# A diffusion layer on one core: the FFN's sums of weights move from VectorE to adding transfers

## The chip, the cores and the metric

The program runs on one core of a Trainium2 chip. A core has a matrix engine (PE, TensorE), a vector engine (DVE, VectorE), a scalar engine (ACT, ScalarE), a general engine (POOL, GpSimd) and a queue engine (SP, SyncE) that here only starts transfers. Sixteen DMA engines carry all transfers of the core. Weights lie in DRAM, tiles in SBUF (128 partitions), products in PSUM. The metric is the device time of one execution in microseconds, as the median of several runs.

## The reference, cut to what matters

One layer is computed for 384 tokens (128 context tokens, 256 latent tokens) of width 2048, all in float32. After a mixing half, which the change doesn't touch, comes a dense SwiGLU feed-forward part (FFN) with 5632 hidden columns:

```python
h = rmsnorm(x, lw['norm_pre_ffn']) * (1.0 + sc2) + sh2
ff = (jax.nn.silu(h @ lw['w_ffn_gate']) * (h @ lw['w_ffn_up'])) @ lw['w_ffn_down']
x = x + ga2 * rmsnorm(ff, lw['norm_post_ffn'])
```

## The kernel before, in words

**Precision.** A float32 product is made of three products of a shorter format (float32r): every operand is split in a high part `hi`, a rounded copy, and a low part `lo = x - hi`, and the kernel forms hi·hi + hi·lo + lo·hi. For weights, ACT makes `whi` (a cast, line 1385) and DVE makes `wlo` (a subtraction, line 1396). Each such weight piece is 128 partitions x 1024 floats, 512 KB.

**The FFN.** The hidden columns are taken in 11 chunks (`NFC`) of 512 columns. The first chunk is made plainly. For chunks 1 to 10 the tokens form three blocks of 128, and the gate and up products of blocks 1 and 2 are made by a scheme of Strassen's kind: seven products of sums of weights with sums of activations instead of eight products. Block 0 is made plainly. The activation sums (`S1` to `S4`) are made once; the weight sums are made for every chunk. A chunk consists of *kinds* of steps, each of four steps i = 0..3 (one quarter of the half of the inner length that the kind works on):

| kind | weights that it multiplies | products of 512 columns in a step |
|---|---|---|
| A | up weights, first half of the inner length | 12 |
| B | gate weights, first half | 12 |
| C | gate weights, second half | 12 |
| E | C - (B - A) | 6 |
| F | C - B | 6 |
| G | up weights, second half | 12 |
| H | G - (C - (B - A)) | 6 |
| D | down weights of the chunk before (eight steps) | 18 |

The list `steps` (line 1308) writes out their order by hand. Before, it is A0..A3, B0..B3, then four times C, E, D, then four times F, G, H, D.

**Where the weights lie.** The pieces of C, G and D are loaded into `raw`, which has two buffers. Those of A and B are loaded into eight places `slots`, tiles named `u...` (shown as `u` in the profile): `x`, the place of A(i), and `y`, the place of B(i). Sums are made in place: x becomes B - A (`sum1`, line 1369), then C - x (line 1392), then G - x (line 1395); y becomes C - y (line 1393). E and H multiply what stands in x, F what stands in y. When F and H have been split, their places are free for the next chunk's loads.

**Order of the work.** For every step, `grab2` takes the split weights of the step from the list `ready`, starts loads (`load_more`: SP, lines 1355 and 1363), and splits the weights of a later entry (`split_next`: the ACT cast, then up to three pending evictions, then the sums, then the DVE subtraction). `whi` and `wlo` have four buffers each, one in use and three ahead: a step's cast can begin when the product step four places ahead of it in the list has ended. All engines execute their instructions strictly in the program's order. SP, too, waits in order: a load into `raw` or into a place waits until DVE has made the `wlo` that read the old contents. A further generator, `ada_last`, loads 64 pieces of 256 KB in the same stage (line 1422) and multiplies them on DVE (line 1427).

Of the kernel before, what the change touches and what calls it, by code (L numbers as in the profile page):

```python
# [15 lines left out]
ALU = mybir.AluOpType  # L16
# [5 lines left out]
D = 2048  # L22
# [12 lines left out]
FC = 4  # L35
NFC = FT // FC
G = 1024
# [59 lines left out]
def tile_step(ctx: ExitStack, tc: tile.TileContext, a, o):  # L97
    nc = tc.nc
    PE, ACT, DVE, POOL, SP = nc.tensor, nc.scalar, nc.vector, nc.gpsimd, nc.sync
# [74 lines left out]
    def down_src(c, n, kh):  # L174

        return a["w_d"][c, 2 * n : 2 * n + 2, :, 512 * kh : 512 * kh + 512].rearrange("i p x -> p i x")
# [429 lines left out]
    with ExitStack() as s:  # L606
# [203 lines left out]
        for c in range(2):  # L810

            dst = a2.rearrange("p (h d j) -> p d h j", d=2, j=P)[:, c]
            raw, up = (x.rearrange("p (h j) -> p h j", j=P) for x in (raw3[1 + c][0:98, 0:512], part[0:98]))
# [28 lines left out]
    with ExitStack() as s:  # L842
# [158 lines left out]
        for b, i in mix_order:  # L1001
# [9 lines left out]
            else:  # L1011
# [3 lines left out]
                p = psm.tile([P, T], F32, tag="mm", name="pmm")  # L1015
                gemm(p, grab(hold=True), oT, 8)
                g, y = gates.pop((b, i))
# [14 lines left out]
    with ExitStack() as s:  # L1032
# [49 lines left out]
        for i in range(KT):  # L1082
            p = psm.tile([P, T], F32, tag="mm", name="pmm")
            for g in range(2):
                n = 2 * i + g - 2 * KT
# [164 lines left out]
        for q in range(2):  # L1250
# [12 lines left out]
        slots = [t[:, n, :] for t, k in (  # L1263
            (actp.tile([P, 3, G], F32, tag="C_hi", name="u012"), 3), (actp.tile([P, 3, G], F32, tag="C_lo", name="u345"), 3),
            (adap.tile([P, 2, G], F32, tag="adacc", name="u67"), 2),
        ) for n in range(k)]
# [41 lines left out]
        steps = []  # L1308
        for c in range(1, NFC):
            steps += [("A", c, i) for i in range(4)] + [("B", c, i) for i in range(4)]  # L1310
            for i in range(4):
                steps += [("C", c, i), ("E", c, i), ("D", c - 1, i)]
            for i in range(4):
                steps += [("F", c, i), ("G", c, i), ("H", c, i)] + ([("D", c - 1, 4 + i)] if c < NFC - 1 or i < 2 else [])
        steps += [("D", NFC - 2, 6 + i) for i in range(2)]
        d_order = (0, 2, 1, 3)
        steps += [("D", NFC - 1, 2 * n + k) for n in d_order for k in range(2)]
# [1 line left out]
        def gu_src(kind, c, half, i):  # L1319
            return a["w_" + kind][FC * c : FC * c + FC, half, :, 256 * i : 256 * i + 256].rearrange("n p x -> p n x")  # L1320

        def src_of(kind, c, i):
            if kind == "D":
                return down_src(c, i // 2, i % 2)
            return gu_src(*{"A": ("u", c, 0), "B": ("g", c, 0), "C": ("g", c, 1), "G": ("u", c, 1)}[kind], i)
# [16 lines left out]
        def slot(x, c, i):  # L1342

            return 4 * ((c + x) % 2) + i
# [19 lines left out]
                resident.pop(0)  # L1364
                kept -= 1

        def sum1(c, i):
            x, y = (slots[slot(n, c, i)] for n in range(2))
            DVE.tensor_sub(x, y, x)  # L1369

        def settle_pend():
            for _ in range(3):
                if pend:
                    pend.pop(0)()

        def split_next():

            if not entries:
                settle_pend()
                return  # L1380
            kind, c, i, raw = entries.pop(0)
            x, y = (slots[slot(n, c, i)] if kind not in "RD" else None for n in range(2))
            src = raw if kind in "RCGD" else y if kind == "F" else x
            hi, lo = (wp.tile([P, G], F32R, tag=t, name=t, bufs=4) for t in ("whi", "wlo"))
            ACT.copy(hi, src)  # L1385
            settle_pend()
            if (kind, i) == ("A", 3):
                sum1(c, 0)
            elif kind == "B" and i < 3:
                sum1(c, i + 1)  # L1390
            elif kind == "C":
                DVE.tensor_sub(x, raw, x)
                DVE.tensor_sub(y, raw, y)
            elif kind == "G":
                DVE.tensor_sub(x, raw, x)
            DVE.tensor_sub(lo, src, hi.bitcast(F32))  # L1396
            if kind in "RCGD":
                out_now[0] -= 1
            elif kind == "F":
                free.add(slot(1, c, i))  # L1400
            elif kind == "H":
                free.add(slot(0, c, i))
            ready.append((hi, lo))

        def grab2(kept=2):
            w = take()
            while now:
                now.pop(0)()
            load_more(kept)
            split_next()  # L1410
            return w
# [52 lines left out]
        for u in range(HEAD):  # L1464
            kind, c, j = ffn_order[u]
            dst_of[kind](hp[u], c, j)
        n = 0
        for kind, c, j in ffn_order[HEAD:]:
            p = psm.tile([P, T], F32, tag="mm", name="pmm")
# [98 lines left out]
        for kind, c, i in steps:  # L1568
# [8 lines left out]
            if kind == "D":  # L1577
                w = grab2()
                n, kh = i // 2, i % 2
# [57 lines left out]
        n = d_order[-1]  # L1637
# [144 lines left out]
```

## Time and profile before

| what | before |
|---|---|
| median of 3 runs | 1968.85 us (1968.83 to 1969.1) |
| the profiled execution | 1969.33 us |
| its span, first to last instruction | 1967.6 us |
| first to last step of chunks 1 to 10 | 973.7 to some 1913 us of the span, 94 us per chunk |
| PE busy, whole span | 1951.9 us (99%) |
| DVE busy | 1620.2 us (82%) |
| ACT busy | 905.7 us (46%) |
| POOL busy | 32.2 us (2%) |
| moved by DMA | 380.08 MB, 193 GB/s on the mean |

The span is the profiled execution between its first and last instruction; the rest, 1.7 us, lies around it. "Busy" counts the time in which an engine executes something; a wait line "A <- B" says that A's engine stood idle until B released it. In a table of windows, the columns after the window are its length, then for each engine the busy time and the number of instructions, then the granted clock of PE (1.00 is full), the mean busy share of the 16 DMA engines and what they moved.

### The profile page before, as it was taken

To read this page: it belongs to the slowest core of one execution; us is meant where nothing else is said; L and a number is where in the kernel's file an instruction comes from. 1 tells how busy PE (TensorE), PEld (TensorE's weight loads), DVE (VectorE), ACT (ScalarE), POOL (GpSimd) and SP (SyncE) were. 2 spreads that over 40 slices of the span, in tenths; PEclk is the share of its full clock that TensorE was granted. 3 is DMA by queue.
4 is the path that set the end of the run, shared out by engine and by line. 5 is a ranking of instruction groups with operands and counts; after the bars stand their busy time and mean duration, and the time that the engine had idled before them with its cause. 6 is when DMAs were issued, how large, how long until landed. Compare 5 with 4: busy or idle time off the path is not lost.

```text
span 1967.6 us, 27720 instructions
## 1 busy us (share of the span) xinstructions
PE 1951.9 (99%) x10704; PEld 1731.7 (88%) x10704; DVE 1620.2 (82%) x2043; ACT 905.7 (46%) x1265; POOL 32.2 (2%) x44
## 2 busy tenths in 40 slices
PE   8999999999999999999999999999999999999998
PEld 6779999999999999999988888888888888888886
DVE  5569788878767778877789998999898999887875
ACT  4233454544345645446454444444444444444444
POOL 0000000000000000004000000000000000000001
PEclk9999999999999999999999999999999999999999
DMA  9978677767755697655345445463636363626243
GB/s 388 372 257 275 211 255 238 234 218 246 238 183 182 197 312 222 196 171 203 119 136 186 149 140 162 154 188 118 193 127 205 100 209 103 208 75 193 75 161 128
DMA packets 189412, 380.08 MB, mean 193 GB/s; under 512 B 14172, under 2 KB 112668, under 8 KB 184928
## 3 DMA queue, kind: packets, MB, share of 16 engines
q1 hardware_dynamic: 189136, 377.92, 59.0%
q8 instruction: 84, 1.38, 0.3%
q14 instruction: 48, 0.39, 0.1%
q10 hardware_dynamic: 144, 0.39, 0.1%
HBM read 361.48 MB, written 16.78 MB: 192 GB/s over the span
## 4 chain that ended last, share of the span: by engine, by line
PE 96%; DMA 1%; DVE 1%; ACT 1%; issue 0%; SPq 0%; POOL 0%; DVEq 0%; ACTq 0%; POOLq 0%
PE pmm L252 35%; PE pgu L1484 30%; PE pdn L1484 18%; PE pv L392 3%; PE pf L252 2%; PE pgm L375 1%; DMA slab<-in_w_ada 1%; PE px L410 1%; PE pmm L1238 1%; PE ptr L1545 1%; PE po L639 1%; DMA raw<-in_w_d 0%; PE pr L574 0%; PE dl L639 0%; PE pp L869 0%; PE px L883 0%
## 5 line engine op out<-in xcount | busy, mean ns | idle before, releaser
L252 PE MATMUL pmm<-A_hi,whi 128*128 128x384 f32 x1200 | 404.2, 337 | 0.0
L252 PE MATMUL pmm<-A_hi,wlo 128*128 128x384 f32 x1200 | 401.3, 334 | 0.0
L252 PE MATMUL pmm<-A_lo,whi 128*128 128x384 f32 x1200 | 401.2, 334 | 0.0
L1385 ACT CAST whi<-u 128x1024 fp32r<-128x1024 f32 x200 | 210.6, 1053 | 275.7 <-DVE u L1369 86.2
L1385 ACT CAST whi<-raw 128x1024 fp32r<-128x1024 f32 x175 | 184.2, 1053 | 209.7 <-DMA raw<-in_w_g 69.8
L218 ACT CAST whi<-raw 128x1024 fp32r<-128x1024 f32 x181 | 189.9, 1052 | 182.4 <-DMA raw<-in_w_gate 59.6
L219 DVE TENSOR_TENSOR wlo<-raw,whi 128x1024 fp32r<-128x1024 f32 x179 | 218.0, 1222 | 66.9 <-ACT whi L218 66.5
L1396 DVE TENSOR_TENSOR wlo<-u,whi 128x1024 fp32r<-128x1024 f32 x200 | 244.2, 1221 | 29.3 <-ACT whi L1385 16.7
L1484 PE MATMUL pgu<-whi,A_hi 128*128 128x512 f32 x640 | 250.0, 391 | 0.0
L1484 PE MATMUL pgu<-whi,A_lo 128*128 128x512 f32 x640 | 249.3, 389 | 0.0
L1396 DVE TENSOR_TENSOR wlo<-raw,whi 128x1024 fp32r<-128x1024 f32 x175 | 213.5, 1220 | 32.3 <-ACT whi L1385 22.7
L252 PEld LDWEIGHTS pmm<-A_hi,whi 128*128 128x128 f32 x1200 | 225.3, 188 | 2.5 <-issue 1.4
L252 PEld LDWEIGHTS pmm<-A_lo,whi 128*128 128x128 f32 x1200 | 225.4, 188 | 0.2
L252 PEld LDWEIGHTS pmm<-A_hi,wlo 128*128 128x128 f32 x1200 | 225.3, 188 | 0.0
L566 DVE SCALAR_TENSOR_TENSOR adacc<-adaw,spad,adacc 128x1024 f32<-128x1024 f32 x180 | 222.8, 1279 | 1.0 <-DMA adaw<-in_w_ada 0.7
L1484 PE MATMUL pdn<-whi,hid_hi 128*128 128x512 f32 x480 | 186.9, 389 | 0.0
L1484 PE MATMUL pdn<-whi,hid_lo 128*128 128x512 f32 x480 | 186.8, 389 | 0.0
L1484 PE MATMUL pgu<-wlo,A_hi 128*128 128x512 f32 x640 | 184.2, 389 | 0.0
L1484 PEld LDWEIGHTS pgu<-whi,A_hi 128*128 128x128 f32 x640 | 120.1, 188 | 26.1 <-issue 0.8
L1484 PEld LDWEIGHTS pgu<-wlo,A_hi 128*128 128x128 f32 x640 | 120.1, 188 | 25.4
L1484 PEld LDWEIGHTS pgu<-whi,A_lo 128*128 128x128 f32 x640 | 120.2, 188 | 25.0
L1484 PE MATMUL pgu<-whi,S 128*128 128x512 f32 x480 | 131.1, 395 | 0.0
(363 smaller groups left out, 2790.2 us busy)
## 6 DMA issues: line engine op xcount, KB each, us to landing
adaw<-in_w_ada SPq DMA_DIRECT2D x96, 512.0 KB, 4.2
raw<-in_w_d SPq DMA_DIRECT2D x88, 512.0 KB, 3.8
slab<-in_w_ada SPq DMA_DIRECT2D x32, 1024.0 KB
raw<-in_w_gate SPq DMA_DIRECT2D x64, 512.0 KB, 4.6
raw<-in_w_g SPq DMA_DIRECT2D x48, 512.0 KB, 3.7
raw<-in_w_u SPq DMA_DIRECT2D x48, 512.0 KB, 4.3
raw<-in_w_in SPq DMA_DIRECT2D x44, 512.0 KB, 3.7
u<-in_w_u SPq DMA_DIRECT2D x40, 512.0 KB, 4.9
```

Of the source, the lines that this page charges most:

```text
L218: ACT.copy(hi, raw)
L219: sub = lambda: eng.tensor_sub(lo, raw, hi.bitcast(F32))
L252: PE.matmul(dst, w[wi][:, k * n + n0 : k * n + n0 + P], x[xi][:, k0 + k, :], start=first and k == 0 and j == 0, stop=last and k == kts - 1 ...
L375: PE.matmul(pgv[q : q + 32, :], spad[:, k, :], slab[k // (KT // 2)][:, k % (KT // 2), :], start=k < 4, stop=k >= KT - 4,)
L392: PE.matmul(pv[2 * t + g], hT[x_][:, kb, t * P : (t + 1) * P], w_[:, g * 512 : (g + 1) * 512], start=kb == 0 and j == 0, stop=kb == KT - 1 ...
L410: PE.matmul(px, w_[:, u * P : (u + 1) * P], hT[x_][:, kb, :], start=j == 0, stop=j == 2)
L566: DVE.scalar_tensor_tensor(acc[:, c, :], w, spad[:, k, c : c + 1], acc[:, c, :], op0=ALU.mult, op1=ALU.add,)
L639: PE.matmul(dst, w[wi], x[xi], start=first and j == 0, stop=last and j == 2)
L1238: PE.matmul(hp[u], hw[u][j][:, ((k - 1) % 8) * P : ((k - 1) % 8 + 1) * P], h2[m][:, k - 1, :], start=k == 1 and j == m == 0, stop=k == KT ...
L1385: ACT.copy(hi, src)
L1396: DVE.tensor_sub(lo, src, hi.bitcast(F32))
L1484: PE.matmul(dst, stat[x_][m], mov(w[w_], m), start=first and w_ == m == x_ == 0, stop=last and w_ == m == 1,)
```

## The change

The 16 DVE subtractions of whole weight pieces in each chunk (4 in `sum1`, 4 + 4 at C, 4 at G) are replaced. ScalarE now changes the sign of the place, and a transfer that GpSimd starts reads the other operand once more from DRAM and adds it to the place in SBUF: x becomes -x, then -x + B, and so on. The sum B - A is begun one entry earlier in the list (at A1, A2, A3 and B0 instead of A3, B0, B1 and B2). In the order of steps, E(i) stands after C(i+1) instead of right behind C(i), and H(i) after G(i+1) instead of right behind G(i).

```diff
@@ -1308,10 +1308,14 @@
             for i in range(4):
-                steps += [("C", c, i), ("E", c, i), ("D", c - 1, i)]
+                steps += [("C", c, i)] + [("E", c, i - 1)] * (i > 0) + [("D", c - 1, i)]
+            steps += [("E", c, 3)]
             for i in range(4):
-                steps += [("F", c, i), ("G", c, i), ("H", c, i)] + ([("D", c - 1, 4 + i)] if c < NFC - 1 or i < 2 else [])
+                steps += [("F", c, i), ("G", c, i)] + [("H", c, i - 1)] * (i > 0)
+                steps += [("D", c - 1, 4 + i)] if c < NFC - 1 or i < 2 else []
+            steps += [("H", c, 3)]
@@ -1364,9 +1368,10 @@
-        def sum1(c, i):
-            x, y = (slots[slot(n, c, i)] for n in range(2))
-            DVE.tensor_sub(x, y, x)
+        def less(x, kind, c, i):
+
+            ACT.mul(x, x, -1.0)
+            POOL.dma_start(x.rearrange("p (n x) -> p n x", n=FC), src_of(kind, c, i), accum_op=ALU.add)
@@ -1384,15 +1389,14 @@
             ACT.copy(hi, src)
             settle_pend()
-            if (kind, i) == ("A", 3):
-                sum1(c, 0)
-            elif kind == "B" and i < 3:
-                sum1(c, i + 1)
+            if kind == "A" and i or (kind, i) == ("B", 0):
+                j = (i - 1) % 4
+                less(slots[slot(0, c, j)], "B", c, j)
             elif kind == "C":
-                DVE.tensor_sub(x, raw, x)
-                DVE.tensor_sub(y, raw, y)
+                less(x, kind, c, i)
+                less(y, kind, c, i)
             elif kind == "G":
-                DVE.tensor_sub(x, raw, x)
+                less(x, kind, c, i)
             DVE.tensor_sub(lo, src, hi.bitcast(F32))
```

## The prediction

> **What bounds the kernel now.** I read the page first, for the engines' shares; then a table of windows over the FFN, one window per chunk; then the waits of PE in that stage.
>
> ```profile
> span 1967.6 us, 27720 instructions
> PE 1951.9 (99%) x10704; PEld 1731.7 (88%) x10704; DVE 1620.2 (82%) x2043; ACT 905.7 (46%) x1265; POOL 32.2 (2%) x44
> ```
>
> ```profile
> core 0: us, PE busy (x) PEld busy (x) DVE busy (x) ACT busy (x) POOL busy (x), PEclk, DMA share, GB/s
> 973.00:1067.00 94.00, 94.00 (x417) 77.97 (x417) 80.30 (x84) 47.99 (x56) 0.00 (x0) 1.00 0.52 160
> 1067.00:1161.00 94.00, 94.00 (x422) 77.81 (x421) 85.63 (x93) 43.17 (x47) 0.00 (x0) 1.00 0.50 154
> ...
> 1819.00:1913.00 94.00, 94.00 (x428) 77.97 (x427) 78.97 (x83) 41.66 (x44) 0.00 (x0) 1.00 0.32 100
> 1913.00:1968.00 55.00, 45.58 (x229) 37.48 (x227) 28.91 (x58) 24.67 (x54) 5.88 (x6) 0.98 0.42 155
> ```
>
> ```profile
> PE py L1662 <- DVE psums L1651: 1.6, 1, 1.6
> PE py L1662 <- ACT psums L1649: 0.8, 3, 0.3
> PE pdn L1484 <- DVE hidE L1547: 0.4, 1, 0.4
> ```
>
> The reader is to see that in the ten chunks PE is busy 94.00 of 94.00 us at full clock, and that between 950 and 1960 us it waits 2.8 us in all, nowhere in these chunks. DVE is the next engine, at 79 to 88 us of 94, but it is never what PE waits for. PE alone sets the time of this stage. So work taken from DVE is worth nothing there; what counts is whether the sums still come in time.
>
> **What the removed work is worth.** These groups (count, busy us, mean ns, idle time before) are the 16 x 10 subtractions:
>
> ```profile
> L1392 DVE TENSOR_TENSOR u<-raw,u 128x1024 f32<-128x1024 f32 x40 | 48.8, 1221 | 17.0 <-DMA raw<-in_w_g 17.0
> L1369 DVE TENSOR_TENSOR u<-u,u 128x1024 f32<-128x1024 f32 x40 | 48.8, 1219 | 0.0
> L1393 DVE TENSOR_TENSOR u<-raw,u 128x1024 f32<-128x1024 f32 x40 | 48.8, 1219 | 0.0
> L1395 DVE TENSOR_TENSOR u<-raw,u 128x1024 f32<-128x1024 f32 x40 | 48.7, 1218 | 0.0
> L1385 ACT CAST whi<-u 128x1024 fp32r<-128x1024 f32 x200 | 210.6, 1053 | 275.7 <-DVE u L1369 86.2 <-PE pgu L1484 56.1 <-DVE u L1395 47.3
> L1385 ACT CAST whi<-raw 128x1024 fp32r<-128x1024 f32 x171 | 180.0, 1053 | 205.6 <-DMA raw<-in_w_g 68.0 <-PE pgu L1484 60.1 <-PE pdn L1484 50.7
> L1396 DVE TENSOR_TENSOR wlo<-raw,whi 128x1024 fp32r<-128x1024 f32 x173 | 211.1, 1220 | 32.3 <-ACT whi L1385 22.7 <-PE pdn L1484 9.3
> ```
>
> DVE loses 195 us, 19.5 per chunk; gain on the path 0, since PE has no idle time there to give back. ACT's waits on `u` from DVE (86.2 us and more) go too, also at 0: three splits lie ahead of PE. At C, `raw` is free 2 x 1.22 = 2.4 us sooner, so its next load may start sooner by as much.
>
> **ACT's change of sign.** 16 per chunk over 128x1024. The trace has none; the nearest row is the cast of the same shape, 1.05 us, so 16.8 us per chunk on top of 43, 60 of 94. Cover: ACT's idle time. If it were gone, the price would be 1.05 us each; bounds 0 and 168 us in all. I take 0, but the delay counts: a C step's two sign changes stand ahead of the next cast, 2.1 us. The sign change at C also waits for the landed B - A, the one at G for the split of E.
>
> **The transfers.** 160 more, 512 KB each: 84 MB on 380. Their pieces have the shape of the loads into the places:
>
> ```profile
> u<-in_w_u SPq DMA_DIRECT2D x40, 512.0 KB, 4.9
> u<-in_w_g SPq DMA_DIRECT2D x40, 512.0 KB, 5.3
> ```
>
> They stand on POOL's queue, which is empty in this stage (0.00 busy above), so they pass nothing there; on the 16 DMA engines they share with SP's loads, whose order doesn't change (C, D, C, D as before). They are in order: x then y. What is queued behind a late one is the next one; who waits is the ACT cast of E, F or H, and behind that cast on ACT the casts of D and of the next C, and that C's sign changes. Then SP: a place is reloaded only after that split.
>
> A chunk moves 154 GB/s at a DMA share of 0.50, so 308 GB/s per full share, and 0.524 MB costs 1.70 us of all 16 engines. An add also has to fetch the old tile before it writes; no row shows such a transfer. From below 1.70 us (the tile's read runs beside the source's), from above 3.40 us (both go through the same engines, one after the other). A gain is excluded, since the bytes are new. I take 3.40, because the tile's bytes equal the source's and the share counts engines' time, not DRAM's.
>
> The Trainium skill, "Collectives: The Full Stack", section "The bandwidth ceiling: the fold count and why AG ≠ RS ≠ AR", says that a reduction in the DMA engines runs at about half the rate of a copy because the add needs two source reads. No run here shows it yet; by it the sum would be the one below, against no change at 1.70 us.
>
> **When they are due.** The step lengths come from the timeline of one chunk (start, duration): A0, C0, E0, D0, C1, then the cast of C3 and the PE steps C2 and C3.
>
> ```profile
> 1066.40 0.39 PE L1484 MATMUL pgu<-whi,A_hi 128*128 128x512 f32 x1
> ...
> 1089.62 0.39 PE L1484 MATMUL pgu<-whi,A_hi 128*128 128x512 f32 x1
> ...
> 1092.34 1.07 PE L1484 MATMUL pgu<-whi,S 128*128 128x512 f32 x4
> ...
> 1093.70 0.39 PE L1484 MATMUL pdn<-whi,hid_hi 128*128 128x512 f32 x1
> ...
> 1097.78 0.39 PE L1484 MATMUL pgu<-whi,A_hi 128*128 128x512 f32 x1
> ...
> 1105.94 0.39 PE L1484 MATMUL pgu<-whi,A_hi 128*128 128x512 f32 x1
> 1106.34 1.05 ACT L1385 CAST whi<-raw 128x1024 fp32r<-128x1024 f32 x1 [3.56 <-DMA raw<-in_w_g]
> 1114.10 0.39 PE L1484 MATMUL pgu<-whi,A_hi 128*128 128x512 f32 x1
> ```
>
> C is 2.72 us, E 1.36, D 4.08, a round 8.16; A and B together 23.22 (8 x 2.72, and three sets of transposes of 0.49). The cast of C3 begins with step C2, three steps ahead. Let C0 start at 0 in the new order C0 D0 C1 E0 D1 C2 E1 D2 C3 E2 D3 E3. E3 starts at 4 x 2.72 + 3 x 1.36 + 4 x 4.08 = 31.3; its low part is first needed four products later (+0.9), and cast and subtraction take 1.05 + 1.22, so its x must have landed by 29.9. C0's cast begins with B1, at -9.1; x0 is negated by -7.0. In these 36.9 us seven sums must pass (x0 y0 x1 y1 x2 y2 x3). The four of B - A come before, the first ready at -26.6 (cast of A1 with the step before H3, at -28.7, plus 2.1).
>
> How much of the DMA engines is free:
>
> ```profile
> 1061.00:1067.00 6.00, 6.00 (x28) 4.99 (x27) 5.93 (x9) 3.23 (x5) 0.00 (x0) 1.00 0.30 100
> 1067.00:1090.00 23.00, 23.00 (x109) 19.01 (x108) 23.00 (x26) 10.94 (x15) 0.00 (x0) 1.00 0.18 53
> 1090.00:1119.50 29.50, 29.50 (x132) 24.44 (x131) 24.77 (x25) 12.63 (x13) 0.00 (x0) 1.00 0.51 155
> ```
>
> Until C0, 0.82 is free: the four B - A need 13.6 us and have 0.82 x 19.6 = 16.1; they fit. Then 7.0 x 0.82 + 29.9 x 0.49 = 20.4 us are free, and the seven need 7 x 3.40 = 23.8. They end 3.4 us late, and PE stands that long ahead of E2 or E3. After that, four sums in 38 us have room, so it doesn't grow. Ten chunks: 34 us. At 1.70 us they need 11.9 of 20.4 and all is hidden; it decides at 2.91 us.
>
> **The later place of E and H.** The products are the same in number, 0 us. Without it E(i) would be due D and C (6.8 us) or a whole round (8.2 us) sooner. Places come free one round later: the next B loads have the A and B stages, 23 us, against a landing of 5.3. Price 0; without that cover, a landing per chunk.
>
> **Sum.** 1969.3 (profiled execution; 0.5 above the median of the runs) + 0 (DVE) + 0 (ACT) + 34 = 2003.
>
> **Rivals.**
>
> *The adds are hidden.* An add costs nearer 1.70 us than 3.40, POOL keeps up, and each E, F, H cast finds its sum landed. For it: 5.3 us landing against a budget of 36.9 / 7 = 5.3 us per sum even if they went one by one, and PE's three steps ahead. Against it: that budget is just used up, with nothing for the tile's read. Time 1969. By the Trainium skill, "DMA: Bandwidth & Descriptors", section "Anatomy of one DMA — SWDGE (gpsimd) path", a transfer started by GpSimd takes about 2.0 us plus its bytes at 436 GB/s; estimated from that, 3.2 us, or 4.4 with the bytes twice, both under that budget, so this rival. No run here shows one.
>
> *POOL is the bound.* GpSimd itself must write the transfer's pieces: 128 partitions x 4 runs of 1 KB, for source, tile and result 1536. Nothing in the trace prices that. The nearest rows are POOL's elementwise ones:
>
> ```profile
> L1168 POOL TENSOR_TENSOR Clo<-t,Clo 128x384 f32<-128x384 f32 x8 | 8.1, 1030 | 2.2 <-DVE t L1164 2.2
> L219 POOL TENSOR_TENSOR wlo<-raw,whi 128x1024 fp32r<-128x1024 f32 x2 | 4.8, 2418 | 0.0
> ```
>
> (2418 - 1030) / 640 = 2.17 ns per column; one piece in that time makes 3.3 us + 0.2 fixed = 3.5, twice that time 6.9. Eleven sums from -26.6 to 29.9 have 56.5 us: it decides at 5.1 us per sum. At 6.9 they end 11 x 6.9 - 56.5 = 19.4 us late, ten chunks 194 us: 2163; 16 x 6.9 = 110 us is then also more than a chunk. For it: a doubling of a weak estimate is enough. Against it: the estimate itself lies below.
>
> *Faster.* That would need over 3.9 us of PE's idle time, and the only idle time near is the 9.4 us in the last window, behind the last chunk, which no edit touches.
>
> **How the numbers follow.** Late by DMA engines 0.45, with its own range 1973 to 2040 (at 2.91 us nothing, at 4 us each 76); POOL the bound 0.26; hidden 0.27; faster 0.02. The range goes from 1967, for the hidden case, to 2150, which leaves out the upper half of the POOL case, the faster case and little else. Within 0.2% (about 4 us, what a measurement of this kernel can tell from no change) is 0.27, slower 0.71.
>
> **What would show it.** Right: a chunk of about 97.4 us, PE idle ahead of E behind `whi`, ACT's casts of `u` waiting for a transfer into `u`, DMA share in the C stage near 1, DVE near 67 us per chunk, 464 MB. Hidden: PE 94.00 of 94.00 again, and E's casts released by PE. POOL's case: its queue never empty from A1 on, chunks of over 100 us, and DMA share well below 1. What would make me wrong: the adds slow SP's loads of `raw`, on which the C casts wait even now (68.0 us), or a sum's latency rather than its rate decides.

## The result, and the profile after

The changed kernel takes 2095.86 us (median of 4 runs, 2089.63 to 2104.38) against 1968.84 us (4 runs). The ratio is 1.0647 [1.0634, 1.0659]: 127 us slower. I had forecast 34 us, with a range that reaches to 2150. The profiled execution (2089.63 us) is the fastest of the four, so its growth is smaller than 127 us.

The head of the page, the DMA queues, and three tables of windows: the stages of chunk 4 before (A and B; C, E and D; F, G, H and D), the same stages after, and the ten chunks with their tail after (columns as in the prediction).

```profile
span 2087.8 us, 28205 instructions
PE 1992.0 (95%) x10704; PEld 1738.4 (83%) x10704; DVE 1445.4 (69%) x1883; ACT 1043.4 (50%) x1425; POOL 238.9 (11%) x204
...
q1 hardware_dynamic: 189136, 377.92, 54.3%
q0 software_dynamic: 84480, 83.90, 25.7%
```

```profile
1255.30:1278.50 23.20, 23.20 (x110) 19.17 (x109) 23.16 (x28) 7.31 (x9) 0.00 (x0) 1.00 0.19 57
1278.50:1311.10 32.60, 32.60 (x145) 27.04 (x144) 30.77 (x32) 16.57 (x20) 0.00 (x0) 1.00 0.51 151
1311.10:1350.10 39.00, 39.00 (x186) 31.88 (x185) 34.54 (x40) 18.33 (x19) 0.00 (x0) 1.00 0.69 218
```

```profile
1292.80:1318.30 25.50, 24.94 (x110) 19.88 (x109) 23.31 (x30) 14.11 (x17) 5.38 (x5) 0.96 0.78 165
1318.30:1356.10 37.80, 34.62 (x146) 27.92 (x145) 19.84 (x21) 22.10 (x25) 10.11 (x8) 0.95 1.05 223
1356.10:1400.40 44.30, 40.12 (x185) 31.51 (x184) 27.62 (x32) 19.66 (x23) 5.14 (x4) 1.00 0.92 243
```

```profile
971.00:2030.00 1059.00, 980.24 (x4261) 783.50 (x4259) 665.77 (x752) 563.75 (x622) 205.28 (x159) 0.98 0.91 211
```

Counted off by the steps' matmuls, a chunk from A0 to the next A0 took 106.5 us on the mean of nine, where it took 94.2: A and B 25.3 us instead of 23.2, the C stage 36.2 instead of 32.6, and the stage from F0 on 45.0 instead of 38.4. So the stage from F0 on, where the sums at G are made, grew most. PE is no longer gapless, and the clock granted to it is below 1.00 in places. Span less PE's busy time was 1967.6 - 1951.9 = 15.7 us before and is 2087.8 - 1992.0 = 95.8 now. The growth of 120.2 us is thus 80.1 us more idle time and 40.1 us more busy time for the same 10704 matmuls. DVE lost 175 us of work, and nothing came of it.

What PE waits for in the FFN (engine and line, releaser: us in all, times, longest):

```profile
PE pgu L1488 <- ACT whi L1390: 34.6, 18, 3.7
PE pdn L1488 <- DVE hid_lo L1551: 17.1, 8, 4.1
PE pgu L1488 <- DVE wlo L1400: 8.8, 16, 1.3
PE pdn L1488 <- DVE psums L1566: 7.2, 7, 2.0
```

One step further back, what ACT's casts wait for in the same stage:

```profile
ACT whi L1390 <- DMA u<-in_w_u: 94.0, 21, 8.2
ACT whi L1390 <- DMA u<-in_w_g: 78.7, 44, 4.3
ACT whi L1390 <- DMA raw<-in_w_d: 78.4, 43, 3.5
ACT whi L1390 <- DMA raw<-in_w_g: 77.0, 27, 5.8
ACT whi L1390 <- DMA raw<-in_w_u: 67.4, 25, 6.2
```

The largest is the transfer into `u` from the up weights: the sums at G, which H needs. By the order of the casts, 66.8 of these 94.0 us, ten waits, are H3's. Of the 78.7 us behind the gate weights 52.3 are B's casts, which wait for B - A, and 25.7 are E3's. The plain loads of `raw` have become late as well: ACT waits 222.8 us for them in the last three rows, and 90.3 in the same stage before. The issue part of the page shows it (transfers, KB each, median us from issue to landing), before:

```profile
raw<-in_w_d SPq DMA_DIRECT2D x88, 512.0 KB, 3.8
...
raw<-in_w_g SPq DMA_DIRECT2D x48, 512.0 KB, 3.7
```

and after, where the first row is 120 of POOL's 160 sums:

```profile
u<-in_w_g POOLq DMA_DIRECT2D x120, 512.0 KB, 8.5
...
raw<-in_w_d SPq DMA_DIRECT2D x88, 512.0 KB, 6.4
...
raw<-in_w_g SPq DMA_DIRECT2D x48, 512.0 KB, 5.3
```

The end of one chunk in the timeline (start, duration; in brackets the idle time before and its releaser). The list stands at G3, H2, D7, H3:

```profile
1058.66 1.05 ACT L1373 ACTIVATE u<-u 128x1024 f32<-128x1024 f32 x1
...
1060.16 1.30 POOL L1374 DMA_DIRECT2D u<-in_w_u  x1 [13.66 <-ACT u L1373]
...
1061.07 1.05 ACT L1390 CAST whi<-raw 128x1024 fp32r<-128x1024 f32 x1 [0.41 <-DMA raw<-in_w_d]
...
1070.27 1.04 ACT L1390 CAST whi<-u 128x1024 fp32r<-128x1024 f32 x1 [8.16 <-DMA u<-in_w_u]
...
1071.37 0.50 PE L1488 MATMUL pgu<-whi,A_hi 128*128 128x512 f32 x1 [2.93 <-ACT whi L1390]
```

ACT negates the place, POOL starts the transfer at 1060.16, and H3's cast starts 10.1 us later. In between ACT casts one other piece (1061.07) and then stands 8.16 us. The product steps ahead are used up, and PE stalls for 2.93 us. H3's products were due at 1068.4 (1071.37 - 2.93).

### The profile page after: what moved, and what is told of

Its sections match the earlier page's. It is cut to its first block, busy times and chain, and to the rows that moved or that the text cites. A ratio compares the mean times of both kernels' runs of the same rounds, so it can differ in the third digit from the quotient of the medians.

```text
span 2087.8 us, 28205 instructions
## 1 busy us (share of the span) xinstructions
PE 1992.0 (95%) x10704; PEld 1738.4 (83%) x10704; DVE 1445.4 (69%) x1883; ACT 1043.4 (50%) x1425; POOL 238.9 (11%) x204
## 3 DMA queue, kind: packets, MB, share of 16 engines
q0 software_dynamic: 84480, 83.90, 25.7%
## 4 chain that ended last, share of the span: by engine, by line
PE 50%; issue 33%; POOL 7%; DMA 5%; DVE 2%; ACT 2%; POOLq 0%; SPq 0%; ACTq 0%; DVEq 0%
PE pmm L252 33%; POOL u L1374 7%; PE pdn L1488 3%; PE pv L392 3%; PE pgu L1488 2%; PE pf L252 2%; PE pgm L375 1%; DMA raw<-in_w_d 1%; DMA u<-in_w_g 1%; PE px L410 1%; PE pmm L1238 1%; DVE wlo L1400 1%; ACT whi L1390 1%; DMA u<-in_w_u 1%; DMA raw<-in_w_u 1%
## 5 line engine op out<-in xcount | busy, mean ns | idle before, releaser
L1488 PE MATMUL pgu<-whi,A_hi 128*128 128x512 f32 x640 | 258.9, 404 | 33.0 <-ACT whi L1390 33.0
L1488 PE MATMUL pgu<-whi,A_lo 128*128 128x512 f32 x640 | 255.2, 399 | 0.0
L1488 PE MATMUL pdn<-whi,hid_hi 128*128 128x512 f32 x480 | 191.6, 399 | 30.4 <-DVE hid_lo L1551 17.1
L1374 POOL DMA_DIRECT2D u<-in_w_g x120 | 155.2, 1389 | 503.2 <-ACT u L1373 498.4
L1488 PE MATMUL pgu<-wlo,A_hi 128*128 128x512 f32 x640 | 189.7, 398 | 9.3 <-DVE wlo L1400 8.8
L1373 ACT ACTIVATE u<-u 128x1024 f32<-128x1024 f32 x160 | 164.8, 1055 | 33.7 <-DVE wlo L1400 33.6
```

Of the source, the lines that this page charges most:

```text
L1373: ACT.mul(x, x, -1.0)
L1374: POOL.dma_start(x.rearrange("p (n x) -> p n x", n=FC), src_of(kind, c, i), accum_op=ALU.add)
L1488: PE.matmul(dst, stat[x_][m], mov(w[w_], m), start=first and w_ == m == x_ == 0, stop=last and w_ == m == 1,)
```

## The experiments

The ratios compare with runs of the kernel before on the same chip, with 95% intervals. Unless said otherwise, an edit is shown against the changed kernel; an added helper that stands already in one of the two kernels (`sum1`, `less`) isn't always shown. Four theories stood against each other in the course of them: the new order of steps costs by itself; the adds take the DMA engines' time (rate); single sums land too late for the step that needs them (due time); and ACT's or POOL's own work costs.

### One part at a time: the order, plain transfers, and groups of sums

**e1_order**: the changed kernel's order of steps, the sums on DVE as before.

```diff
-        def less(x, kind, c, i):
-            ACT.mul(x, x, -1.0)
-            POOL.dma_start(x.rearrange("p (n x) -> p n x", n=FC), src_of(kind, c, i), accum_op=ALU.add)
+        def sum1(c, i):
+            x, y = (slots[slot(n, c, i)] for n in range(2))
+            DVE.tensor_sub(x, y, x)
...
-                less(x, kind, c, i)
-                less(y, kind, c, i)
+                DVE.tensor_sub(x, raw, x)
+                DVE.tensor_sub(y, raw, y)
...
-                less(x, kind, c, i)
+                DVE.tensor_sub(x, raw, x)
```

> The new order of steps alone, sums on DVE as before. Whole-chunk theory (an adding transfer takes 3.35 us of all 16 DMA engines, so that a chunk needs 47 + 16 x 3.35 = 101 us of them while PE needs 94): no transfers added, so 1969, within 2 us. Order theory (the later place of E and H itself costs, by places that come free later): some 10 to 40 us more than before.

Measured: 1978.05 us, 1.0047 [1.0032, 1.0062]. The order alone costs 9 us. Its place in the timeline of that kernel, one of three such stalls:

```profile
1283.90 1.04 ACT L1389 CAST whi<-raw 128x1024 fp32r<-128x1024 f32 x1 [7.64 <-DMA raw<-in_w_g]
1284.86 0.58 ACT L1551 CAST hid_hi<-ptr 128x512 fp32r<-128x512 f32 x1
...
1285.47 0.69 DVE L1551 TENSOR_TENSOR hid_lo<-ptr,hid_hi 128x512 fp32r<-128x512 f32 x1 [3.87 <-ACT hid_hi L1551]
...
1286.21 0.50 PE L1488 MATMUL pdn<-whi,hid_hi 128*128 128x512 f32 x1 [2.88 <-DVE hid_lo L1551]
```

At the start of a chunk the list is now C0, D0, C1: three pieces in a row through the two buffers of `raw`, where E0 used to stand between. C1's cast waits 7.64 us for its load, and the cast of the hidden values that D0 needs is queued behind it on ACT. That is why the wait shows as `hid_lo`.

**e2_plain**: all 160 transfers stay, but they copy instead of adding, so the sums are not formed.

```diff
-            POOL.dma_start(x.rearrange("p (n x) -> p n x", n=FC), src_of(kind, c, i), accum_op=ALU.add)
+            POOL.dma_start(x.rearrange("p (n x) -> p n x", n=FC), src_of(kind, c, i))
```

> The changed kernel with plain transfers in place of adding ones: the same bytes from DRAM to the same places, started by GpSimd behind the same changes of sign; the additions are left out, so that the weight sums are not formed. Whole-chunk theory: a transfer costs about 1.7 us of the engines, half of the adding one, a chunk needs 47 + 27 = 74 of 94 us, time 1969 to 1980. GpSimd theory (a transfer started by GpSimd lands late by its own path, whatever it does): stays at 2050 to 2100.

Measured: 1988.57 us, 1.0097 [1.0079, 1.0114], so 11 us beyond the order, and above the 1980 that I had expected at most. Even the copy is awaited by H3's cast: 37.4 us in nine of ten chunks. The queue's row and the landing of its transfers:

```profile
q0 software_dynamic: 23040, 83.90, 12.6%
DMA to landing us min/median/max: 3.9/5.5/8.4
```

12.6% of 16 engines over 1990.1 us is 1.57 us per transfer. In the changed kernel it is 25.7% of 2087.8 / 160 = 3.35 us, and its landing is 5.7/8.7/12.9. The adding makes the transfer 2.14 times as dear and lets it land 3.2 us later; 107 of the 127 us hang on it.

**e3_b_and_g**: only the sums at B and G as transfers, those at C on DVE. **e4_c_only**: only the sums at C. For e3_b_and_g

```diff
-                less(x, kind, c, i)
-                less(y, kind, c, i)
+                DVE.tensor_sub(x, raw, x)
+                DVE.tensor_sub(y, raw, y)
```

and for e4_c_only

```diff
-            if kind == "A" and i or (kind, i) == ("B", 0):
-                j = (i - 1) % 4
-                less(slots[slot(0, c, j)], "B", c, j)
+            if (kind, i) == ("A", 3):
+                sum1(c, 0)
+            elif kind == "B" and i < 3:
+                sum1(c, i + 1)
...
-                less(x, kind, c, i)
+                DVE.tensor_sub(x, raw, x)
```

> Only the sums at B and G (8 of 16 per chunk) are transfers, the C sums are DVE's again. Whole-chunk theory: 47 + 8 x 3.35 = 74 us of 94, so 1969 to 1985. C-stage theory (the prediction's: only the seven sums around C are late): 1969. Late-H theory (the sum at G(3) has the shortest way to its use, H(3), and its landing alone costs a stall in every chunk): 10 x 3 to 6 us, 2000 to 2030.

> Only the 8 sums at C are transfers, those at B and G are DVE's again. Whole-chunk theory: the same 74 us of 94 as the kernel with B and G, and so about the same time, 1969 to 1985. C-stage theory: seven sums in the same 20.4 us of free engine time, so 2000 or more, the larger part of the loss. Late-H theory: 1969.

Measured: e3_b_and_g 2041.65 us, 1.0366 [1.0343, 1.0388]; e4_c_only 2014.83 us, 1.0234 [1.0219, 1.0249]. Each has eight transfers per chunk, so half of the added engine time. My prediction had priced the C stage alone; the sums at B and G cost more (73 against 46 us, the order included in both). A queue by rate doesn't explain that: 47 + 8 x 3.4 = 74 us of engine time fit into a chunk of 94.

### Rate or due time

**e5_old_order**: the changed kernel with the order of steps from before.

```diff
-                steps += [("C", c, i)] + [("E", c, i - 1)] * (i > 0) + [("D", c - 1, i)]
-            steps += [("E", c, 3)]
+                steps += [("C", c, i), ("E", c, i), ("D", c - 1, i)]
...
-                steps += [("F", c, i), ("G", c, i)] + [("H", c, i - 1)] * (i > 0)
-                steps += [("D", c - 1, 4 + i)] if c < NFC - 1 or i < 2 else []
-            steps += [("H", c, 3)]
+                steps += [("F", c, i), ("G", c, i), ("H", c, i)] + ([("D", c - 1, 4 + i)] if c < NFC - 1 or i < 2 else [])
```

> The changed kernel with the order of steps from before: E(i) right behind C(i), H(i) right behind G(i). Rate theory (the engines' work per chunk, 47 + 16 x 3.35 = 101 us, sets the time): the same bytes and sums, so 2085 to 2110. Late-sum theory (a sum that lands some 8.5 us after its start holds ACT in order, and PE stalls as soon as three splits don't cover that): every E and H cast now waits for a sum begun just before, eight times per chunk some 6 us more; 2250 to 2500.

Measured: 2409.24 us, 1.2235 [1.2215, 1.2256]. Same bytes, same adds, 313 us more. Waits of ACT and PE, and one window over the stage:

```profile
ACT whi L1386 <- DMA u<-in_w_u: 385.7, 40, 11.8
ACT whi L1386 <- DMA u<-in_w_g: 341.2, 67, 9.6
...
PE pgu L1484 <- ACT whi L1386: 244.9, 73, 6.2
```

```profile
1000.00:1950.00 950.00, 744.75 (x2903) 578.24 (x2903) 462.37 (x534) 384.12 (x428) 139.37 (x108) 0.89 0.75 167
```

All 40 sums at G are now waited for, 9.6 us each, while the DMA engines are only 0.75 busy. With engine time to spare on the mean, lateness of single sums makes the time. PE's clock (0.89) falls too.

**e7_packed**: the same sums from weights laid out so that a piece is 4 KB in a row per partition instead of four runs of 1 KB.

```diff
-            return a["w_" + kind][FC * c : FC * c + FC, half, :, 256 * i : 256 * i + 256].rearrange("n p x -> p n x")
+            return a["w_" + kind + "p"][c - 1, half, i].rearrange("p (n x) -> p n x", n=FC)
```

> The changed kernel with the gate and up weights of chunks 1 to 10 laid out so that a piece is 4 KB in a row for each partition instead of 4 x 1 KB; the same bytes. If the adding transfer costs by bytes (source and tile, 2 x 1.7 us): still 3.3 us of the 16 engines per sum, time within 25 us of the changed kernel. If it costs by packets (528 of 1 KB, against 144 of 4 KB for the plain one): about 1.6 to 2.2 us per sum, and the time falls to 1980 to 2010.

Measured: 2070.54 us, 1.0516 [1.05, 1.0531]. The first row is the queue's, the second a window over the ten chunks and the stage's tail:

```profile
q0 software_dynamic: 23040, 83.90, 22.4%
```

```profile
971.00:2010.00 1039.00, 976.25 (x4262) 784.48 (x4260) 663.31 (x752) 561.97 (x622) 137.32 (x159) 0.98 0.84 215
```

A sum costs 22.4% of 2067.6 / 160 = 2.89 us, less by 0.46, with 144 packets each instead of 528. With as few packets as the copy it is still 1.84 times as dear (2.89 against 1.57), so most of its price doesn't go by the number of packets. The engines' whole work in this window is 0.84 x 1039 = 873 us, under the 940 that ten chunks took before, and the kernel is still 101 us slower.

**e8_g3_dve**: the changed kernel, with one sum of the 16, G(3)'s, back on DVE.

```diff
-                less(x, kind, c, i)
+                less(x, kind, c, i) if i < 3 else DVE.tensor_sub(x, raw, x)
```

> The changed kernel, but of the 16 sums of a chunk the one at G(3), whose use H(3) follows it at the shortest distance, is made by DVE. Rate theory: 15 of 16 transfers, 47 + 50 us, so some 3.4 us per chunk less at most, 2060 to 2090. Late-sum theory: the wait of ACT for G(3)'s sum (7 to 8 us in every chunk) goes, with it the stall of PE ahead of A(0) (2 to 3.7 us) and what its low clock costs; 2035 to 2065.

Measured: 2045.91 us, 1.0388 [1.0372, 1.0403]: 50 us less for a sixteenth of the transfers. PE's wait for `whi`:

```profile
PE pgu L1488 <- ACT whi L1390: 14.3, 12, 2.4
```

It was 34.6 us. H3 stands three places behind G3. Other sums have a reader as near in the list (E0, E3 and B's casts), but by the records of the changed kernel G(3)'s has the least time: 6.1 us on the median from its start to the moment when H3's cast would have had to begin, against a landing of 8.6. It lands later than that in nine of ten chunks, the other 150 sums of the stage in two cases.

**e9_order_h**: the kernel before with only the later place of H.

```diff
-                steps += [("F", c, i), ("G", c, i), ("H", c, i)] + ([("D", c - 1, 4 + i)] if c < NFC - 1 or i < 2 else [])
+                steps += [("F", c, i), ("G", c, i)] + [("H", c, i - 1)] * (i > 0)
+                steps += [("D", c - 1, 4 + i)] if c < NFC - 1 or i < 2 else []
+            steps += [("H", c, 3)]
```

> The kernel before with only the later place of H; E stands right behind C as before; sums on DVE. If the 9 us of the new order come from C(0), D(0) and C(1) standing in a row (three pieces through two raw buffers, and the cast of the hidden values for D queued on ACT behind that of C(1)): 1969. If they come from places that come free later (H a round later): 1974 to 1980.

Measured: 1969.9 us, 1.0005 [0.9995, 1.0014]. No difference, so the order's 9 us belong to C, E and D.

### Single sums on the order of before

**e10_g3_only**: e9_order_h, with G(3)'s sum as a transfer, ten in all. **e12_g012**: the other three at G. **e13_b_only**: the kernel before, with the four B - A as transfers, begun where the changed kernel begins them. The first two edits are against e9_order_h, the third against the kernel before; the helper `less` comes in addition:

```diff
-                DVE.tensor_sub(x, raw, x)
+                less(x, kind, c, i) if i == 3 else DVE.tensor_sub(x, raw, x)
```

```diff
-                DVE.tensor_sub(x, raw, x)
+                less(x, kind, c, i) if i < 3 else DVE.tensor_sub(x, raw, x)
```

```diff
-            if (kind, i) == ("A", 3):
-                sum1(c, 0)
-            elif kind == "B" and i < 3:
-                sum1(c, i + 1)
+            if kind == "A" and i or (kind, i) == ("B", 0):
+                j = (i - 1) % 4
+                less(slots[slot(0, c, j)], "B", c, j)
```

> The kernel before with the later place of H, and one sum in a chunk, the one at G(3), as an adding transfer. Step lengths: from the change of sign at G(3) to where H(3)'s cast must begin lie 6.8 + 8.2 - 1.5 - 2.1 = 11.4 us, less what G(3)'s own load is late (2.7 us on the mean of its waits). If a sum lands in 6 to 7 us when the DMA engines are little loaded, it is covered: 1969 to 1974. If its way by itself is too long (landing 8.5 as in the changed kernel): 10 x 2 to 4 us, 1985 to 2010.

> The kernel before with the later place of H, and the sums at G(0), G(1) and G(2) as adding transfers, 30 in all. Distance to H(i) is longer than that of G(3). Late-sum theory: all hidden, 1969 to 1972, though DVE has 3.7 us less per chunk. Rate theory: 3 x 3.35 = 10 us of the engines in 38 us that have 11.4 free, hidden as well.

> The kernel before, order and all, with only the four sums B - A as adding transfers (40 in all), begun at A(1), A(2), A(3) and B(0). They are due some 19 us later, at C. Late-sum theory: hidden, 1969 to 1973. Rival (added traffic delays the loads of B and C that fall in the same 23 us): 1980 to 2000.

Measured: e10_g3_only 1989.76 us, 1.0102 [1.0087, 1.0117]; e12_g012 1971.32 us, 1.0009 [1.0, 1.0019]; e13_b_only 1969.59 us, 1.0001 [0.9992, 1.0011]. Ten transfers cost 20 us, thirty others 2, and forty others nothing that can be told. The landing of the ten is 6.8/9.5/10.4 us (min/median/max). ACT's waits for them, and the window around one:

```profile
ACT whi L1392 <- DMA u<-in_w_u: 62.5, 10, 7.0
```

```profile
1050.00:1062.00 12.00, 12.00 (x54) 9.93 (x54) 6.91 (x8) 3.18 (x5) 1.43 (x1) 1.00 0.93 248
```

ACT waits for every one, 6.3 us on the mean. There is no queue of other sums here; the sum lands late by itself, in a stretch in which SP's own loads keep the engines 0.93 busy, though the stage's mean is 0.51. PE itself stands only 0.3 us ahead of H3: it has 12.3 us on the median from the sum's start to H3's last moment, more than the landing. What it waits for comes behind, when ACT and DVE have fallen back, in short waits of the next steps:

```profile
PE pgu L1491 <- DVE wlo L1403: 5.6, 14, 0.6
```

The thirty and the forty are awaited too, but each for a shorter time (e12_g012, then e13_b_only):

```profile
ACT whi L1392 <- DMA u<-in_w_u: 22.8, 12, 3.4
ACT whi L1390 <- DMA u<-in_w_g: 33.1, 23, 3.1
```

The forty show who reads B - A. My expectation, like the table ahead of the prediction, has it due at C. In the code (`src` in `split_next`) the cast of a B step takes its weights from `x`, which holds B - A by then, so the reader is B's own cast, three places after the sum's start. It is hidden even so.

**e11_settle_first**: the changed kernel with the pending evictions ahead of the cast. It tests a theory of mine at that point, that the order of work on ACT (a waiting cast with evictions behind it) makes the cost.

```diff
-            ACT.copy(hi, src)
             settle_pend()
+            ACT.copy(hi, src)
```

> The changed kernel with the pending evictions, the casts of the hidden values among them, put ahead of the weight's cast on ACT and DVE instead of behind it. Theory of the order on ACT (D(0) waits for hidden values whose cast stands behind that of C(1), which waits for its load): the stalls of PE behind the subtraction of the hidden values (17 us idle, and the low clock behind them) go, 2060 to 2080. Rival (these stalls only show a lateness that comes from the sums and would show elsewhere): 2085 to 2105.

Measured: 2106.67 us, 1.0694 [1.0676, 1.0711]. That theory falls: the time rises by 11 us. PE's stalls behind `hid_lo` are replaced by longer ones behind `whi` (42.9 us at gate and up, 9.5 at down) and `psums` (17.9).

### The last four: the other sums, the ones that are hidden taken together, and the sign

**e14_y_only**: the kernel before, with the sums of y (C - B) as transfers. **e15_x_only**: the new order, with the sums of x at C as transfers. **e16_far_ones**: the later place of H, and 11 of the 16 sums per chunk, all but x at C and G(3): four B - A, four y, G(0) to G(2); its edits are those of e13_b_only, e14_y_only and e12_g012 together. The first edit is e14_y_only's, the second stands for e15_x_only; both are shown as edits of the DVE sums (for e15_x_only beside the changed kernel's order of steps):

```diff
-                DVE.tensor_sub(y, raw, y)
+                less(y, kind, c, i)
```

```diff
-                DVE.tensor_sub(x, raw, x)
+                less(x, kind, c, i)
```

> The kernel before, order and all, with only the four sums C - B (in y) of a chunk as adding transfers. They are due at F, a round or more later. Late-sum theory (only a sum that is due soon costs): hidden, 1969 to 1972. Traffic theory (adding transfers in the C stage make the loads of raw land late, whenever the sum is due): 1980 or more.

> The kernel with the new order (1978 by itself), with only the four sums in x at C as adding transfers; E uses each one round later. Late-sum theory: the larger part of the 37 us that the C sums cost beyond the order, 1990 to 2010. Traffic theory: half the transfers, half of the cost, 1990 or less, as for y.

> The kernel before with the later place of H, and 11 of the 16 sums as adding transfers: B - A (four), y at C (four), G(0) to G(2). Only those due soon, x at C and G(3), stay on DVE. The engines' work per chunk is 47 + 11 x 3.35 = 84 of 94 us. Late-sum theory: the parts B and G(0) to G(2) cost 0 and 2 us alone, so 1970 to 1985 together with y. Traffic theory: more than half of the 127 us that all sixteen cost, 2030 and up.

Measured: e14_y_only 1970.71 us, 1.0007 [0.9998, 1.0017]; e15_x_only 2006.57 us, 1.0191 [1.0176, 1.0206]; e16_far_ones 1973.36 us, 1.002 [1.001, 1.003]. The stage of e16_far_ones in one window, and its queue:

```profile
973.00:1913.00 940.00, 938.67 (x4242) 774.76 (x4241) 722.15 (x801) 526.86 (x571) 139.52 (x109) 1.00 0.85 208
```

```profile
q0 software_dynamic: 58080, 57.68, 19.2%
```

Eleven of the sixteen sums, 110 transfers and 110 changes of sign, cost 4 us: PE is busy 938.67 of 940 us with the engines at 0.85. ACT waits 152.0 us for loads of `raw` there, against 90.3 before, so slower loads up to that are hidden too.

E's four x cost 28 us beyond the order, the four y nothing that can be told, although the engines were busier in the C stage with y (0.80, by windows over nine chunks) than with x (0.68). What ACT waits for with x:

```profile
ACT whi L1394 <- DMA u<-in_w_g: 61.6, 17, 6.1
```

By the order of the casts, 47.3 of these 61.6 us are E3's, in nine of ten chunks. E3 stands three places behind C3, as H3 behind G3. PE doesn't stand ahead of E3 here; it waits 11.2 us behind `hid_lo` ahead of D0, as in e1_order (5.5). A kernel with only C(3)'s sum on DVE was not tried.

**e6_sign**: the new order, ACT's change of sign, and the addition on DVE from SBUF, no transfer.

```diff
-            POOL.dma_start(x.rearrange("p (n x) -> p n x", n=FC), src_of(kind, c, i), accum_op=ALU.add)
+            DVE.tensor_add(x, y, x)
...
-                less(x, kind, c, i)
-                less(y, kind, c, i)
+                ACT.mul(x, x, -1.0)
+                DVE.tensor_add(x, raw, x)
+                ACT.mul(y, y, -1.0)
+                DVE.tensor_add(y, raw, y)
```

> The new order with ACT's changes of sign and DVE additions of what lies in SBUF, no added transfers. ACT has 16.9 us more per chunk, as in the changed kernel, DVE its 19.5 again. If ACT's share in the loss is its own work: 1990 or more. If it is hidden as I took it: the 1978 of the new order, within 4 us.

Measured: 2025.7 us, 1.0289 [1.0273, 1.0304]. Read as I had expected it (1990 or more), this would speak for ACT's own work as a cost. But the kernel makes a new wait that the changed kernel doesn't have: DVE's additions stand in order behind ACT's changes of sign. So it doesn't decide.

```profile
DVE u L1398 <- ACT u L1397: 64.8, 32, 5.4
```

That ACT's own work is cheap rests on two other kernels: in e16_far_ones 11 of the 16 changes per chunk are hidden, and e2_plain has all 16, and 160 transfers as well, for 11 us beyond the order.

## Why the prediction was wrong, step by step

**PE bounds the FFN; work taken from DVE is worth nothing: right.** e16_far_ones takes 110 subtractions, 134 us at 1.22, from DVE and gains nothing.

**ACT's change of sign at 0: right as far as shown**, for the 110 of e16_far_ones; all 160 cost at most the 11 us of e2_plain there.

**The price of an adding transfer, 3.40 us of all 16 engines: right.** It measured 3.35, and 3.35 to 3.49 in the other kernels with the same pieces, against 1.57 for the copy. The Trainium skill, "Collectives: The Full Stack", section "The bandwidth ceiling: the fold count and why AG ≠ RS ≠ AR", has half the rate for a reduction between cores; 3.35 / 1.57 = 2.14 here is near it. The 464 MB came as forecast.

**When they are due: this is the step that failed.** It priced one queue by rate, the seven sums at C, and put the sums at G at nothing with "After that, four sums in 38 us have room, so it doesn't grow". But the stage from F0 on grew most, by 6.6 us per chunk. A sum has a due time of its own, and from its start to its landing it takes 8.7 us on the median and 5.7 at the least. In the timeline of H3 above, the products were due at 1068.4 and the cast 1.05 before; so G(3)'s sum had 7.2 us from its start at 1060.16, more than the 5.3 of the plain landing that I had quoted, and less than it takes. e8_g3_dve gives back 50 us for this one sum, and e10_g3_only has 20 us for it with no other sum beside it. My own last sentence named this ("a sum's latency rather than its rate decides"), but no step priced it.

Which sums cost is told by how long ACT waits for a single one. The runs with one group each, on the kernel before or with the order alone:

| sums as transfers | landing, min/median/max, us | ACT's waits: times, mean, longest | cost, us |
|---|---|---|---|
| y at C (e14_y_only) | 5.7/7.6/8.9 | none | 0 to 3 |
| B - A (e13_b_only) | 5.7/6.1/8.6 | 23, 1.4, 3.1 | about 0 |
| G(0) to G(2) (e12_g012) | 6.9/8.9/10.3 | 12, 1.9, 3.4 | 2 |
| x at C (e15_x_only) | 5.7/6.6/10.0 | 17, 3.6, 6.1 | 28 beyond the order |
| G(3) (e10_g3_only) | 6.8/9.5/10.4 | 10, 6.3, 7.0 | 20 |

As far as these runs go, short waits are covered by the three splits that lie ahead of PE, and the long ones of E3 and H3 are not.

**The C stage: a near number by luck.** I had forecast 34 us there, with PE standing ahead of E2 or E3. e4_c_only has 37 us beyond the order, and the C stage of the changed kernel grew by 3.6 us per chunk with its engines at 1.05 in the window above, full as forecast. But PE hardly ever stands ahead of an E; it stands ahead of D0 (17.1 us behind `hid_lo`). And by the rate the four x alone would be hidden (4 x 3.40 = 13.6 of 20.4 us), while e15_x_only has 28 us for them.

**The four B - A: a wrong reader, at no cost.** They were taken as due at C. The 86.2 us that ACT waits for line 1369 in the profile before are B's casts, so B reads them, as the code says. In the A and B stage they land in 6.1 us on the median and are hidden.

**A missing term: the slower products after a stall.** 40.1 of the 120.2 us are more busy time. The pages of the experiments give idle and busy growth in a like ratio:

| kernel | span growth, us | more PE idle | more PE busy |
|---|---|---|---|
| changed kernel | 120.2 | 80.1 | 40.1 |
| e5_old_order | 438.7 | 289.5 | 149.2 |
| e7_packed | 100.0 | 64.3 | 35.7 |
| e8_g3_dve | 78.4 | 50.5 | 27.9 |
| e4_c_only | 47.3 | 32.4 | 14.9 |
| e10_g3_only | 20.6 | 12.1 | 8.5 |

So each us of stall came with about half a us more, from 0.29 in e1_order to 0.78 in e15_x_only. Part of it is the granted clock, 0.999 on the mean before and 0.988 after, by an estimate 2087.8 x 0.011 = 23 us (its trace is in the last section); what makes up the other 17 isn't separated.

**The later place of E and H at price 0: wrong by 9 us, and its worth too small.** H's part costs nothing (e9_order_h), E's 9 us (e1_order), by the timeline there since C0, D0 and C1 now share two buffers. I had looked for what comes free later, not for what comes closer together. What the later places save was told as 6.8 to 8.2 us of due time; in the kernel's time it is 313 us (e5_old_order).

**The loads of `raw`.** That the adds would slow SP's loads was my other sign of being wrong, and they do: ACT's waits for them rise from 90.3 to 222.8 us. At 152.0 us they are hidden (e16_far_ones); what the rest costs isn't separated from the late sums.

**The rivals and the range.** POOL as the bound fell: a sum keeps POOL busy for 1.28 us, the engine is 11% busy. The measured time lies in my range only because of that case; the one that I priced ended at 2040 (its own 76 us make it 2045). Hidden adds fell as a whole, but hold for 11 of 16. The Trainium skill, "DMA: Bandwidth & Descriptors", section "Anatomy of one DMA — SWDGE (gpsimd) path", would by estimate give 3.2 us for the copy and 4.4 with the bytes twice; the landings here are 5.5 and 8.7 on the median, beside other loads, and 3.9 and 5.7 at the least. By the least of the copy it is near, for the adding transfer it is short in every case.

**What stays open.** Rate has a share that I can't separate. The engines' work before is 0.48 of 940 us (451), and 160 x 3.35 more makes 987, while the changed kernel's window has 0.91 x 1059 = 964: by that alone ten chunks couldn't end in 940 us, but 24 to 47 us later. Yet e8_g3_dve with 0.92 x 1019 = 937 us of work and e7_packed with 873 have no such floor, and lose 77 and 101 us. The parts don't add up either: 9 + 28 + 2 + 20 + 0 + 2 = 61 of 127. One link between them is on record: together with the other sums, G3's own load of `raw` lands late (24.6 us of ACT's waits in the changed kernel, none in e10_g3_only), and the time that G(3)'s sum has shrinks from 12.3 us on the median in e10_g3_only to 6.1. That fits the 50 us of e8_g3_dve against the 20 of e10_g3_only. How the rest of the 66 us comes about, and how a wait of ACT becomes time of PE where PE doesn't stand at that step, is not shown. A third buffer for `raw` was not tried.

## What to carry to other kernels

When work on data is moved from an engine to a transfer, check each result singly: find its reader in the code, and set the time from the transfer's start to that reader, in the order of the engine that waits for it, against the whole landing time under the load of that moment; what is short is compared with the lead that the bound engine has. A sum of rates over a stage comes second. One result per chunk that was 6.3 us late for its cast cost 20 us in ten chunks here, though the DMA engines were half idle on the mean. Where the bound engine is already gapless, even the well hidden transfers (11 of 16 here) bring nothing.

## What was not expected of the hardware

Around a stall of 4.05 us the granted clock fell to 0.50. The stall's end in the timeline and the windows around it, with a group of the same six matmuls later:

```profile
1109.21 0.80 PE L1488 MATMUL pdn<-whi,hid_hi 128*128 128x512 f32 x1 [4.05 <-DVE hid_lo L1551]
...
1111.09 2.76 PE L1488 MATMUL pdn<-wlo,hid_hi 128*128 128x512 f32 x6
...
1120.76 1.52 PE L1488 MATMUL pdn<-wlo,hid_hi 128*128 128x512 f32 x6
```

```profile
1107.00:1109.20 2.20, 0.00 (x0) 0.00 (x0) 0.73 (x2) 2.20 (x3) 0.00 (x0) 0.58 1.14 277
1109.20:1112.00 2.80, 2.79 (x7) 2.21 (x8) 1.30 (x2) 2.80 (x5) 2.31 (x2) 0.50 0.72 111
1112.00:1114.00 2.00, 2.00 (x6) 1.60 (x5) 2.00 (x2) 0.70 (x1) 0.28 (x1) 0.50 0.64 175
```

Six matmuls took 2.76 us instead of 1.52. The clock was low already in the stall (0.58 on the mean of its last 2.2 us) and for 4.8 us behind it. Behind the shorter stall at H3 (2.93 us, shown above) it fell as well, two us after the stall's end:

```profile
1073.20:1076.70 3.50, 3.50 (x9) 2.28 (x7) 3.47 (x6) 0.53 (x1) 0.00 (x0) 0.51 0.67 221
```

and behind the one of 2.88 us in e1_order it didn't:

```profile
1288.00:1291.00 3.00, 3.00 (x15) 2.47 (x14) 3.00 (x4) 0.00 (x0) 0.00 (x0) 1.00 0.07 13
```

In the clock's record of the changed kernel, every low stretch between 1000 and 2050 us is 3.41 or 6.83 us long, ten in all, and they begin at multiples of 3.41 us from each other. So where a stall lies on this grid may decide whether the clock falls; that is read from one trace, not tested.

The Trainium skill, "TensorE: Matmul & The Clock Gate", Part 1, has half clock after an idle window of about 3.4 us, until the engine has been busy for about as long. The length of the low stretches agrees. That the idle time must reach 3.4 us does not: the low stretch of the first case began about 2.2 us into the stall, and a stall of 2.93 us in all was enough for the second.

An adding transfer also takes more packets: 84480 for 160 sums, 528 each, against 144 for the copy of the same pieces, and 1.28 us of POOL against 0.75.
